# RWKV block inverses in a hybrid decoder layer: dense matmuls placed between the two groups of first products

## The chip, the cores and the metric

The kernel runs on one core of one Trainium2 chip. The metric is the device time of one execution in microseconds (us), the median of three runs; lower is better. One further execution was recorded by the hardware profiler, and the views of the profile and the trace are of that one. In the views, PE is TensorE (matmuls), PEld its weight loads, DVE is VectorE, ACT is ScalarE, POOL is GpSimd and SP is SyncE; PEclk is the share of full speed that TensorE's clock was granted.

## What is computed

The reference is one decoder layer on 1024 tokens of width 1024: RWKV-7 time mixing and an indexer-selected sparse attention side by side, gated together, then a SwiGLU feed-forward part. The change lies in the time mixing, whose core is a recurrence over the tokens, for 8 heads of 64 channels each:

```python
def step(state, inp):
    r_t, d_t, k_t, v_t, kk_t, a_t = inp
    sa = jnp.einsum('bhij,bhj->bhi', state, -kk_t)
    state = (state * d_t[:, :, None, :]
             + sa[..., None] * (kk_t * a_t)[:, :, None, :]
             + v_t[..., None] * k_t[:, :, None, :])
    y_t = jnp.einsum('bhij,bhj->bhi', state, r_t)
    return state, y_t
```

## The kernel before

The tokens are worked on in two halves of 512. Weights and activations are split into a high and a low part, and a dense product is the sum of three matmuls per 128 rows of the contraction (`mm3`, lines 137 to 149: L142 and L143 with the high part of the weight, L147 with its low part). One such dense matmul covers 128 x 128 weights and 512 tokens. For every weight tile ScalarE makes the high part (L116) and VectorE the low part (L117), after a load of 512 KB (L123).

**The recurrence in chunks.** `rwkv(half, ...)` runs over the quarters q of 256 tokens, two in each half, and each quarter has four chunks of 64 tokens, taken as two pairs (pr), each of two chunks (pa). Inside a chunk the recurrence becomes a triangular system, whose matrix must be inverted for every one of the 8 heads. The 64 x 64 inverse is made of blocks of 32:

1. The matrices MT of all chunks are computed (L710 to L714), and their 32 x 32 diagonal blocks go through memory (`d_n`) into a layout in which one partition holds one block (N).
2. The substitution: a loop of 31 steps on VectorE (L748 to L753) inverts all diagonal blocks. The results go back through memory (`d_w`, L755 and L764) into the tile TT, and VectorE transposes the upper blocks into TZ (L767).
3. First products: for each pair pr, 16 matmuls of 32 x 32 (L781), which the trace records as 32, multiply the off-diagonal block by a diagonal inverse. ScalarE copies the result to TZ with two copies for each pair (L784).
4. `inner(0)` (L791, 32 records; copied by L794 into rhs) is independent of the inverses.
5. Second products (L802): for each pair the copy of step 3 times the other diagonal inverse; ScalarE copies the result with a changed sign into TT (L805). Now the inverse is complete, and the scan over the four chunks begins (L843, L862, L874).

**What fills the time.** TensorE's issue order is the order in which the program is written (`manual_schedule` for PE alone). All other work of TensorE stands in a queue of generators, `fill`. `pump(n)` adds n to a credit and takes steps from the queue until the credit is used up; a step of dense work counts as many credits as it has matmuls (mostly 4, in one order of the feed-forward part 7), so that the credit can fall below zero and the next call then brings less. `ticks(n, m)` pumps n in m parts and after each part takes one step of a second generator, `beside`, the search for the attention's thresholds (L1008, and between its two passes L1030 and L1032). The calls before the first products cover the substitution:

```python
ticks((209, 231, 281, 232)[q], (13, 4, 10, 6)[q])
```

What the filler consists of differs by the quarter: in quarter 0 it is projections and gates (L142 to L147), in quarter 1 attention for the first half (`attend(0)`: logits L1109, their maximum on VectorE L1111, the exponent on ScalarE L1114, transposes L1144, values L1154, the end of a head pair with a store to `d_yb` at L1191) in turn with gates (L516, L517 and a store to `d_g`), in quarter 2 the merging of the branches (L1329, L1331, L248), in quarter 3 the feed-forward part (L1388 to L1392; L160 in its output order). At the start of quarter 2 the queue is emptied completely (`ready`).

**The other engines.** The order of VectorE, ScalarE, GpSimd and the DMA queues is made by a planner, which goes through the program with estimated durations and gives an engine that is free the earliest written instruction that it takes to be ready. On the chip each engine then keeps this order, so that an instruction that waits holds up all behind it. Small temporaries (`tmp`) rotate through four buffers: an instruction that writes a new one waits until the buffer's last user is done, which can be a store. Products that are not dense go to five PSUM banks (`mix`), dense ones to three (`acc`).

Of the kernel before, what the change touches and what calls it, by code (L numbers as in the profile page):

```python
# [51 lines left out]
def block_kernel(ctx: ExitStack, tc: tile.TileContext, ins: dict, outT: bass.AP, outR: bass.AP, stop=None, dbg=None):  # L52
# [56 lines left out]
    def mix():  # L109
        return psM.tile([128, HT], F32, tag="mix", name="mix")  # L110
# [66 lines left out]
    def pump(n):  # L177

        credit[0] += n
        while credit[0] > 0 and fill:  # L180
            try:
                credit[0] -= abs(next(fill[0]))
            except StopIteration:
                fill.popleft()
        if not fill:
            credit[0] = 0
# [3 lines left out]
    def ticks(n, m):  # L190

        for i in range(m):
            pump(n * (i + 1) // m - n * i // m)
            next(beside[0], None)
# [353 lines left out]
    def rwkv(half, p, consts, ready=None, settled=None):  # L548
# [5 lines left out]
        for q in range(2 * half, 2 * half + 2):  # L554
# [217 lines left out]
                             d_bs[q][e].rearrange("c s -> (c s)").partition_broadcast(64))  # L772
            bon = v
            G.tensor_tensor(bon, v, bsp, op=ALU.mult)
            ticks((209, 231, 281, 232)[q], (13, 4, 10, 6)[q])
            both = [(h, pa, 64 - 64 * pa, 64 * pa) for h in range(8) for pa in range(2)]
            hd = [(h, h // 2, slice((h % 2) * 64, (h % 2) * 64 + 64), slice(h * 64, h * 64 + 64)) for h in range(8)]
            for pr in range(2):
                ps = mix()
                for h, pa, ba, kb in both:  # L780
                    T.matmul(ps[ba + 32:ba + 64, h * 32:(h + 1) * 32], MT[2 * pr + pa][ba:ba + 32, h, ba + 32:ba + 64],  # L781
                             TZ[ba:ba + 32, 0, pr, h, :], start=True, stop=True)
                for ba in (64, 0):
                    A.activation(TZ[ba + 32:ba + 64, 1, pr, :, :],  # L784
                                 ps[ba + 32:ba + 64, 0:256].rearrange("p (h t) -> p h t", h=8), AF.Copy)

            def inner(pr):
                ps = mix()
                for h, pa, ba, kb in both:
                    hc = hd[h][3]  # L790
                    T.matmul(ps[ba:ba + 64, hc], MT[2 * pr + pa][kb:kb + 64, h, ba:ba + 64],  # L791
                             UV[pr][kb:kb + 64, pa, hc], start=True, stop=True)
                rhs = p.tile([128, 512], F32, tag="rhs", name="rhs")
                A.activation(rhs, ps, AF.Copy)  # L794
                return rhs
# [956 lines left out]

    fill.append(att0())
    rwkv(0, rp, consts)
    zps, z0, f0, merging = [], [], [], []

# [10 lines left out]
    def settled():  # L1767

        next(merging[0])
        fill.append(chain(merging[0], ffn(0, zps[0][1], z0, f0)))  # L1770

    rwkv(1, rp, consts, ready, settled)
    wq[0] = SY
    sz0, zp0 = zps[0]
# [114 lines left out]
```

## Time and profile before

| what | value |
|---|---|
| median of three runs | 1706.21 us (1706.05 to 1706.52) |
| profiled execution | 1709.14 us, of it 1707.2 us span from the first to the last instruction |
| TensorE busy | 1686.1 us, 99% of the span |
| VectorE, ScalarE, GpSimd busy | 1180.9, 896.4, 97.3 us |
| mean granted clock of TensorE | 0.996 |
| first products of quarters 0 to 3 begin at | 426.5, 575.5, 739.4 and 895.0 us |

The times in all rows of the timeline are us from the start of the span: start, busy time, engine, line, operation, output and inputs, shapes and count, and in brackets the engine's idle time just before with what ended it. Rows merge equal instructions that follow each other, and a matmul's busy time includes the part in which the next one already runs, so that rates are read from starts. In a view by stretches, each engine has its busy time and, in brackets, its instructions, and then come the granted clock, the share of the DMA engines and the GB/s. In the view of waits a row has the total, the number and the longest.

### The profile page before, as it was taken

Reading aid. Unit: us, or ns where it says so; the run is one execution under the profiler, and the core shown is the slowest. Engines: PE = TensorE matmul, PEld = TensorE weight load, DVE = VectorE, ACT = ScalarE, POOL = GpSimd, SP = SyncE. Lnnn points to the kernel's source line nnn. Section 1 sums busy time; section 2 is a strip of 40 time slices with the busy share of each in tenths; the row PEclk is TensorE's granted clock in tenths of the full one; section 3 lists DMA queues with packets and bytes.
Section 4 is the critical chain, followed back from the end, with each engine's and each line's share of the span. In section 5 each row is a group of like instructions: output and inputs, shape, how many; then the busy total and the mean of one; then the engine's idle time right before and its main releaser. Section 6 shows DMA issues by size and latency. Waiting matters only on the chain.

```text
span 1707.2 us, 28295 instructions
## 1 busy us (share of the span) xinstructions
PE 1686.1 (99%) x10802; PEld 1419.4 (83%) x10802; DVE 1180.9 (69%) x2305; ACT 896.4 (53%) x1727; POOL 97.3 (6%) x107
## 2 busy tenths in 40 slices
PE   9999999999999999999999999999999999999998
PEld 8888888878878777878787888878888899899998
DVE  6789889967567458957886655535564885675764
ACT  6365998453554588755334365533323544353452
POOL 0000000000021110000200110000000000000002
PEclk9999999999999899999999999999999999999999
DMA  6542334436257525653343633244455344524532
GB/s 220 178 136 91 98 104 149 147 108 181 98 177 213 153 95 170 207 171 109 106 123 97 213 128 120 76 154 166 145 185 187 113 156 131 183 95 144 169 113 99
DMA packets 142231, 243.58 MB, mean 143 GB/s; under 512 B 48864, under 2 KB 71072, under 8 KB 141968
## 3 DMA queue, kind: packets, MB, share of 16 engines
q1 hardware_dynamic: 119360, 170.76, 31.3%
q10 hardware_dynamic: 16128, 48.60, 8.5%
q0 software_dynamic: 6608, 22.42, 4.2%
q8 instruction: 85, 1.39, 0.3%
q14 instruction: 50, 0.41, 0.1%
HBM read 188.73 MB, written 53.00 MB: 142 GB/s over the span
## 4 chain that ended last, share of the span: by engine, by line
PE 87%; DVE 5%; DMA 3%; ACT 2%; issue 1%; POOL 1%; SPq 0%; ACTq 0%; POOLq 0%; DVEq 0%
PE acc L142 18%; PE acc L147 18%; PE acc L143 18%; PE acc L160 3%; PE mix L1597 3%; PE mix L1595 3%; PE mix L1594 3%; PE mix L1154 2%; PE mix L958 2%; PE mix L1144 2%; PE mix L1128 1%; PE acc L417 1%; DVE wlo L117 1%; PE mix L142 1%; PE acc L1597 1%
## 5 line engine op out<-in xcount | busy, mean ns | idle before, releaser
L117 DVE TENSOR_TENSOR wlo<-wst,whi 128x1024 fp32r<-128x1024 f32 (+1 forms) x203 | 246.4, 1216 | 181.2 <-PE acc L147 73.9
L116 ACT ACTIVATE whi<-wst 128x1024 fp32r<-128x1024 f32 (+1 forms) x203 | 212.3, 1048 | 185.7 <-PE acc L143 137.1
L142 PE MATMUL acc<-zhi,whi 128*128 128x512 f32 x400 | 158.8, 397 | 0.0
L143 PE MATMUL acc<-zlo,whi 128*128 128x512 f32 x400 | 156.1, 390 | 0.0
L142 PE MATMUL acc<-u1hi,whi 128*128 128x512 f32 x320 | 128.5, 401 | 0.0
L143 PE MATMUL acc<-u1lo,whi 128*128 128x512 f32 x320 | 125.5, 392 | 0.0
L142 PE MATMUL acc<-u0hi,whi 128*128 128x512 f32 (+1 forms) x320 | 122.8, 386 | 0.0
L143 PE MATMUL acc<-u0lo,whi 128*128 128x512 f32 (+1 forms) x320 | 121.3, 382 | 0.0
L147 PE MATMUL acc<-zhi,wlo 128*128 128x512 f32 x400 | 103.1, 395 | 0.0
L142 PE MATMUL acc<-fhi,whi 128*128 128x512 f32 x234 | 91.9, 393 | 0.6 <-ACT whi L116 0.5
L143 PE MATMUL acc<-flo,whi 128*128 128x512 f32 x234 | 91.1, 390 | 0.0
L142 PEld LDWEIGHTS acc<-zhi,whi 128*128 128x128 f32 x400 | 75.1, 188 | 16.9 <-issue 1.8
L143 PEld LDWEIGHTS acc<-zlo,whi 128*128 128x128 f32 x400 | 75.2, 188 | 14.7
L147 PEld LDWEIGHTS acc<-zhi,wlo 128*128 128x128 f32 x400 | 73.6, 188 | 15.6 <-issue 1.2
L147 PE MATMUL acc<-u1hi,wlo 128*128 128x512 f32 x320 | 82.5, 398 | 0.0
L147 PE MATMUL acc<-u0hi,wlo 128*128 128x512 f32 (+1 forms) x320 | 78.7, 384 | 0.0
L1008 ACT ACTIVATE junkl<-kept,z 128x1024 int8<-128x1024 int16 (+1 forms) x64 | 69.4, 1084 | 4.6 <-DVE kept L977 4.4
L142 PEld LDWEIGHTS acc<-u1hi,whi 128*128 128x128 f32 x320 | 60.3, 189 | 12.7 <-issue 0.9
L147 PEld LDWEIGHTS acc<-u1hi,wlo 128*128 128x128 f32 x320 | 59.6, 190 | 12.8 <-issue 0.9
L142 PEld LDWEIGHTS acc<-u0hi,whi 128*128 128x128 f32 x320 | 60.2, 188 | 11.9 <-issue 0.4
L143 PEld LDWEIGHTS acc<-u1lo,whi 128*128 128x128 f32 x320 | 60.5, 189 | 11.3
L143 PEld LDWEIGHTS acc<-u0lo,whi 128*128 128x128 f32 x320 | 60.2, 188 | 11.0
(455 smaller groups left out, 4041.0 us busy)
## 6 DMA issues: line engine op xcount, KB each, us to landing
wst<-in_w_ffn_in SPq DMA_DIRECT2D x72, 512.0 KB, 3.8
wst<-in_w_in ACTq DMA_DIRECT2D x36, 512.0 KB, 3.9
wst<-in_w_in SPq DMA_DIRECT2D x25, 512.0 KB, 4.3
wst<-in_w_fo SPq DMA_DIRECT2D x25, 512.0 KB, 3.5
h<-in_xT SPq DMA_DIRECT2D x32, 256.0 KB, 5.2
d_g<-tmp ACTq DMA_DIRECT2D x32, 256.0 KB, 2.8
k<-d_k POOLq DMA_DIRECT2D x16, 512.0 KB, 5.8
tmp<-d_g SPq DMA_DIRECT2D x32, 256.0 KB, 3.0
```

The source lines that it names most:

```text
L116: A.activation(hi, x, AF.Copy)
L117: V.tensor_tensor(lo, x, hi.bitcast(F32), op=ALU.subtract)
L142: T.matmul(ps, whi[:, wk + k, :], ahi[:, ak + k, tok], start=k == 0, stop=False)
L143: T.matmul(ps, whi[:, wk + k, :], alo[:, ak + k, tok], start=False, stop=False)
L147: T.matmul(ps, wlo[:, wk + k, :], ahi[:, ak + k, tok], start=False, stop=k == nk - 1)
L160: T.matmul(ps, w[:, k, :], a[:, k, tok], start=k == 0 and j == 0, stop=k == nk - 1 and j == 2)
L958: T.matmul(ps[:, :w], iq[:, h, :], ik[:, i, c:c + w], start=i == 0, stop=i == 1)
L1008: A.activation(junka[:, :n], y, AF.Sign, bias=z[:, i:i + 1], accum_out=cnt[:, i:i + 1])
L1144: T.transpose(ps[:, j * 128:(j + 1) * 128], L[:, (c + j) * 128:(c + j + 1) * 128], ident)
L1594: T.matmul(ps, whi[:, k, :], ahi[:, k, :], start=opens and k == 0, stop=False, skip_group_check=True)
L1595: T.matmul(ps, whi[:, k, :], alo[:, k, :], start=False, stop=False, skip_group_check=True)
L1597: T.matmul(ps, wlo[:, k, :], ahi[:, k, :], start=False, stop=k == 3, skip_group_check=True)
```

## The change

Two lines. Behind each of the two groups of first products, after its two copies on ScalarE are written, `pump(4)` is called, in every quarter. The pumping before the first products falls from 209, 231, 281 and 232 to 202, 223, 281 and 226, that is by 7, 8, 0 and 6. The number of parts in which it is done stays.

```diff
-            ticks((209, 231, 281, 232)[q], (13, 4, 10, 6)[q])
+            ticks((202, 223, 281, 226)[q], (13, 4, 10, 6)[q])
             both = [(h, pa, 64 - 64 * pa, 64 * pa) for h in range(8) for pa in range(2)]
             hd = [(h, h // 2, slice((h % 2) * 64, (h % 2) * 64 + 64), slice(h * 64, h * 64 + 64)) for h in range(8)]
             for pr in range(2):
                 ps = mix()
                 for h, pa, ba, kb in both:
                     T.matmul(ps[ba + 32:ba + 64, h * 32:(h + 1) * 32], MT[2 * pr + pa][ba:ba + 32, h, ba + 32:ba + 64],
                              TZ[ba:ba + 32, 0, pr, h, :], start=True, stop=True)
                 for ba in (64, 0):
                     A.activation(TZ[ba + 32:ba + 64, 1, pr, :, :],
                                  ps[ba + 32:ba + 64, 0:256].rearrange("p (h t) -> p h t", h=8), AF.Copy)
+                pump(4)
```

No matmul is added or removed: what is pumped at one place is missing from the queue at a later one.

## The prediction

> **What bounds the kernel now.** I read the page first: its busy table, then its chain.
>
> ```profile
> span 1707.2 us, 28295 instructions
> PE 1686.1 (99%) x10802; PEld 1419.4 (83%) x10802; DVE 1180.9 (69%) x2305; ACT 896.4 (53%) x1727; POOL 97.3 (6%) x107
> ...
> PE 87%; DVE 5%; DMA 3%; ACT 2%; issue 1%; POOL 1%; SPq 0%; ACTq 0%; POOLq 0%; DVEq 0%
> ```
>
> TensorE is busy 99% of the span and its issue order is fixed by the program. Every dense matmul is run once in either kernel, so the change can only gain where TensorE stands still or is slowed, and only lose where it adds such time. Hence the view of waits next, for TensorE alone.
>
> ```profile
> PE mix L802 <- ACT TZ L784: 2.7, 3, 2.3
> PE mix L710 <- DVE MT L714: 1.9, 2, 1.1
> ...
> PE mix L781 <- DVE TZ L767: 0.7, 1, 0.7
> ```
>
> The longest of all its waits lies at the place of the change: the second products (L802) wait for the copies (L784) of the first products (L781), once for 2.3 us. The other row that the change can reach is L781 waiting for a transpose. So I read TensorE's timeline at each of the four places. Quarter 0 is the undisturbed pattern:
>
> ```profile
> 425.96 0.39 PE L142 MATMUL acc<-u0hi,whi 128*128 128x512 f32 x1
> 426.19 0.39 PE L143 MATMUL acc<-u0lo,whi 128*128 128x512 f32 x1
> 426.50 1.20 PE L781 MATMUL mix<-TZ,MT 32*32 32x32 f32 x64
> 427.63 1.15 PE L791 MATMUL mix<-UV,MT 64*64 64x64 f32 x32
> 428.71 0.50 PE L142 MATMUL acc<-u0hi,whi 128*128 128x512 f32 x1
> ...
> 429.83 1.20 PE L802 MATMUL mix<-TT,TZ 32*32 32x32 f32 x64
> ...
> 432.00 0.50 PE L142 MATMUL acc<-u0hi,whi 128*128 128x512 f32 x1
> ```
>
> The step from one start to the next is what counts, since the durations overlap: a dense matmul takes 0.23 us (425.96 to 426.19), 64 first products 1.13, the inner products (L791) 1.08, L802 and L843 together 2.17. The four dense ones behind L791 take 1.12 (428.71 to 429.83), not 0.92: going from small products to dense and back costs about 0.2 us.
>
> Quarter 1 holds the long wait, so here TensorE, ScalarE and the granted clock:
>
> ```profile
> 574.23 0.88 PE L1154 MATMUL mix<-pt,v 128*64 128x128 f32 x12
> 575.04 0.50 PE L1109 MATMUL mix<-k,q 128*128 128x256 f32 x2
> 575.47 1.20 PE L781 MATMUL mix<-TZ,MT 32*32 32x32 f32 x64
> ...
> 581.21 2.31 PE L802 MATMUL mix<-TT,TZ 32*32 32x32 f32 x64 [2.33 <-ACT TZ L784]
> ...
> 585.35 0.79 PE L142 MATMUL acc<-u1hi,whi 128*128 128x512 f32 x1
> ```
> ```profile
> 574.54 0.71 ACT L1030 ACTIVATE tmp<-kept,top 128x512 f32<-128x512 int16 x1
> ...
> 576.05 0.51 ACT L1114 ACTIVATE L<-L,mx 128x256 f32<-128x256 f32 x1 [0.80 <-DVE mx L1111]
> ...
> 578.91 1.84 ACT L1030 ACTIVATE tmp<-kept,top 128x512 f32<-128x512 int16 x3 [2.26 <-DMA d_yb<-tmp]
> 580.78 1.57 ACT L784 ACTIVATE TZ<-mix 32x256 f32<-32x256 f32 x4
> ```
> ```profile
> 576.00:580.00 4.00, 2.88 (x79) 2.24 (x72) 0.95 (x4) 1.69 (x4) 0.00 (x0) 1.00 0.99 377
> 580.00:584.00 4.00, 2.71 (x70) 2.51 (x70) 1.44 (x3) 3.84 (x10) 0.00 (x0) 0.58 0.08 26
> 584.00:588.00 4.00, 4.00 (x22) 3.17 (x21) 1.15 (x4) 2.71 (x7) 0.00 (x0) 0.50 0.00 2
> 588.00:592.00 4.00, 4.00 (x27) 3.06 (x28) 0.43 (x2) 3.60 (x10) 1.20 (x2) 0.64 0.23 66
> ```
>
> The first products take their 1.13 us, to 576.6, but their copies begin at 580.78. ScalarE keeps the order that it was given: three L1030 stand ahead of L784, and the first of them waits until 578.91 for a store (d_yb) that has to land before its buffer is free, while the DMA share of that stretch is 0.99. TensorE idles 2.33 us, and then the granted clock falls to half: L802 and L843 take 4.14 us here (581.21 to 585.35) against 2.17 in quarter 0. Lost clock over the three stretches: 4 x (0.42 + 0.50 + 0.36) = 5.1 us, an estimate from above, since TensorE partly stands in it. Bounds for the drop: at least the 2.0 us of those two groups, at most 5.1; I take 4.8, as nearly all that follows until 591 is work at TensorE's own pace.
>
> [...]
>
> Quarter 2 has two smaller stalls:
>
> ```profile
> 739.44 0.75 PE L781 MATMUL mix<-TZ,MT 32*32 32x32 f32 x34
> 740.92 0.69 PE L781 MATMUL mix<-TZ,MT 32*32 32x32 f32 x30 [0.73 <-DVE TZ L767]
> ...
> 745.88 1.11 PE L843 MATMUL mix<-S,AR 64*128 64x64 f32 x16
> ```
> ```profile
> 740.43 0.43 DVE L767 STREAM_TRANSPOSE TZ<-TT 32x256 f32<-32x256 f32 x1 [1.52 <-DMA TT<-d_w]
> ```
> ```profile
> 743.63 1.57 ACT L784 ACTIVATE TZ<-mix 32x256 f32<-32x256 f32 x4
> ```
>
> The second group waits for the last transpose, which waits for its DMA until 740.43; later L802 waits for copies that begin at 743.63. Quarter 3 has no wait at all:
>
> ```profile
> 895.04 1.20 PE L781 MATMUL mix<-TZ,MT 32*32 32x32 f32 x64
> ...
> 897.25 1.88 PE L160 MATMUL acc<-flo,whi 128*128 128x512 f32 x7
> 899.06 1.20 PE L802 MATMUL mix<-TT,TZ 32*32 32x32 f32 x64
> ```
>
> **The change part by part.** No matmul is added or removed. Credits before the first products fall by 7, 8, 0 and 6, and 8 come back behind the two groups, so behind them the filler stands 1, 0, 8 and 2 credits ahead, within its quarter. Three terms.
>
> *New borders.* Each quarter gets two more islands of filler between small products. Price of one: 1.12 - 4 x 0.23 = 0.2 us, the nearest row there is. It is not below zero, since the filler itself costs its usual time. Quarter 0: 0.4. Quarter 2: 0.4. Quarter 3: its filler comes in pieces of seven (L160 x7 above), so 4 + 4 + 4 credits buy two islands where one stood: 0.2. Quarter 1: paid inside the wait for ScalarE, so 0 while that wait is there, 0.4 if it goes. Sum 1.0; its range is 0.5 to 1.4, by half the price and by two islands everywhere.
>
> [...]
>
> *Quarter 2.* The first group starts at 739.44 as before (281 is unchanged) and takes 0.6. Four dense then run to 739.44 + 0.6 + 1.1 = 741.1; the second group's transpose ends at 740.86, so its wait is covered with 0.3 us to spare. Second group 0.6, four dense 1.1, inner products 1.1, four dense 1.1: L802 is reached at about 745.1. By the quoted ScalarE row all four copies end at 745.20 and the first pair at 744.4, so both groups find theirs. L843 then starts at 746.2 instead of 745.88, 0.3 later, but with eight dense matmuls more behind it, worth 8 x 0.23 = 1.8: a gain of 1.5 us, islands already paid. Without the cover (transpose or copies later by over a microsecond) it falls towards the bare islands, -0.4.
>
> *Quarter 1.* Filler here is attention as well as dense work. L1154 and L1109 carry 3 and 2 credits and the two pieces ahead of them 4 each, so seven credits fewer take out just those two items: L781 starts about 1.2 us earlier, with L1154 behind the first group and L1109 behind the second. TensorE still has the same work ahead of L802 and reaches it near 579.2. ScalarE's row decides: L1030 is written ahead of L784 in both kernels and the planner takes ready work in that order, so the copies remain behind the store that lands at 578.91. L802 starts near 581.2 as before: 0.
>
> *What could be uncovered.* Starting L781 up to 8 x 0.23 = 1.8 us sooner needs its transposes:
>
> ```profile
> 423.09 0.42 DVE L767 STREAM_TRANSPOSE TZ<-TT 32x256 f32<-32x256 f32 x1
> ...
> 566.64 1.35 DVE L767 STREAM_TRANSPOSE TZ<-TT 32x256 f32<-32x256 f32 x3
> ...
> 890.46 0.42 DVE L767 STREAM_TRANSPOSE TZ<-TT 32x256 f32<-32x256 f32 x1
> ```
>
> They end at 423.5, 568.0 and 890.9; L781 would start at 424.7, 574.3 and near 893.4. All hold, quarter 0 by 1.2 us. No semaphore wait is added, but copies of the second group are now written behind four credits of filler, so ScalarE may place that filler's work ahead of them; they have over 3 us until L802 in quarters 0 and 3. Filler's own weight loads, splits and stores on the ScalarE and SyncE queues keep their order and move by up to 1.8 us against the inverse. Behind the second quarter the filler runs 8 credits ahead, which shifts its VectorE bursts against the next norms; the waits there (L710, 1.9 us in two) can grow or shrink by about a microsecond, and I take 0.
>
> Sum: +0.4 (quarter 0) + 0 - 1.5 (quarter 2) + 0.2 (quarter 3) = -0.9 us. The islands of quarter 2 are inside its -1.5. The profiled execution took 1709.14 us, 1.9 beyond its span; with the sum it would take 1708.2. The median of the three runs is 2.9 us lower, 1706.21, and so the forecast is 1705.3. Whether those runs have the clock drop is not shown; they agree within 0.5 us, so probably all or none.
>
> **The rivals.**
>
> *A, the copies get past L1030.* L1030's first one was started while L1114 was not ready, and then L1114 was placed ahead of the rest, so the rest may not have been ready in the planner's eyes. With L781 1.2 us earlier, L784 can take that slot; if both pairs do, wait and drop go: -0.9 + 0.4 - 2.3 - 4.8 = -7.6, 1698.6 us. For it: ScalarE's gap at 576.05. Against: the second pair is written behind the filler. 0.17.
>
> *B, wait stays, clock doesn't fall.* TensorE reaches L802 near 579.2, so it idles 1.9 instead of 2.33 us: -0.9 - 4.8 = -5.7, 1700.5 us. The trace halves the clock after 2.33 us and does not after 0.73 (quarter 2), so 1.9 lies between, nearer to the first. [...] 0.13.
>
> *C, slower: copies of the second group late in another quarter.* If ScalarE sets the shifted filler, or a wait like L1030's, ahead of them, L802 waits there and the clock falls. The copies of a pair take 0.8 us and L802 comes 3.3 us after its group, so it decides from 2.5 us of delay on; quarter 1 shows that 4 us occur. Price as in quarter 1, 2.3 + 4.8: 1705.3 + 7.1 = 1712.4 us. 0.12.
>
> *D, no cover in quarter 2* (its stalls are not in every run, or move along): bare islands, +1.0, 1707.2 us. 0.10.
>
> **How the numbers follow.** The forecast gets 0.48. 0.2% of this time is 3.4 us, about what a measurement of this kernel can tell from no change. Faster by more: A and B, 0.30. Within: forecast and D, 0.58. Slower: C, 0.12. The forecast's own range is 1703.8 to 1707.6, by the bounds of the islands and a microsecond at the norms; the range for 8 in 10 takes in B and reaches to A, about half of which it leaves out with C: 1699.0 to 1708.5.
>
> **What would show it.** Right: L781 in two groups of 32 with filler between; quarter 2 without the 0.73 us wait, its L843 with eight more dense behind it at 746; in quarter 1 L1030 still ahead of L784 on ScalarE, L802 near 581 and a clock below 1.00 after it; islands at 1.1 us for four dense. Wrong: the copies directly behind their products in quarter 1, a clock of 1.00 throughout, or L802 waiting in quarter 0 or 3.

## The result and the profile after

The kernel after takes 1723.58 us (median of six runs, 1717.57 to 1725.12), the kernel before on the same chip 1707.3 us (1706.05 to 1710.24): a ratio of 1.0085, 95% interval 1.0066 to 1.0104. It is slower by 16 us, outside the predicted range. The profiled execution took 1723.18 us. Two runs of an experiment and two of the kernel before beside the experiments, of 1848.04 to 9491.47 us, were disturbed (two of them at a granted clock of 0.849) and are left out of all figures. Lines from 787 on are one higher in the kernel after.

The first lines of its page, and its view of waits for TensorE (total, number, longest, in us):

```profile
span 1721.1 us, 28296 instructions
...
PE 1693.6 (98%) x10802; PEld 1422.4 (83%) x10802; DVE 1183.6 (69%) x2305; ACT 899.8 (52%) x1727; POOL 94.8 (6%) x107
```
```profile
PE mix L710 <- DVE MT L714: 2.6, 3, 1.4
PE acc L1350 <- ACT yhi L116: 1.8, 1, 1.8
PE mix L875 <- ACT UV L866: 1.7, 2, 0.9
PE mix L655 <- ACT nrT L649: 1.4, 1, 1.4
...
PE acc L143 <- DVE zlo L117: 1.2, 1, 1.2
PE mix L863 <- DVE rhs L854: 1.2, 1, 1.2
PE mix L255 <- DVE sacc L249: 1.1, 1, 1.1
```

L802 (now L803) and L781, the two rows that the change was about, no longer stand among the long waits. In their place are single waits of 0.9 to 1.8 us at lines that the diff does not touch: the norms (L655, L710), the start of the merge (L1350), the scan (L863, L875) and the feed-forward part (L255, L143).

At the place of the change things went as forecast. TensorE in quarter 2, and the two steps that had stalled it (VectorE's last transposes, ScalarE's copies):

```profile
740.76 0.69 PE L781 MATMUL mix<-TZ,MT 32*32 32x32 f32 x32
741.38 0.50 PE L142 MATMUL acc<-mhi,whi 128*128 128x512 f32 x1
...
742.51 0.69 PE L781 MATMUL mix<-TZ,MT 32*32 32x32 f32 x32
...
746.48 1.20 PE L803 MATMUL mix<-TT,TZ 32*32 32x32 f32 x64
747.61 0.66 PE L844 MATMUL mix<-S,AR 64*128 64x64 f32 x8
```
```profile
739.93 0.90 DVE L767 STREAM_TRANSPOSE TZ<-TT 32x256 f32<-32x256 f32 x2 [2.29 <-DMA TT<-d_w]
```
```profile
743.60 1.57 ACT L784 ACTIVATE TZ<-mix 32x256 f32<-32x256 f32 x4
```

No wait is left. From L781 to L844 it is 6.85 us (747.61 - 740.76), before 6.44 (745.88 - 739.44), with eight dense matmuls more inside: 8 x 0.23 - 0.41 = 1.4 us gained where 1.5 was forecast. But quarter 2 began its inverse 1.3 us later than before, and the profiled execution as a whole lost 13.9 us of span.

Quarter 1, on ScalarE, TensorE and in the stretches behind it (busy times, then granted clock, DMA share, GB/s):

```profile
577.58 1.34 ACT L1031 ACTIVATE tmp<-kept,top 128x512 f32<-128x512 int16 x2 [1.07 <-DMA d_yb<-tmp]
579.17 0.62 ACT L1031 ACTIVATE tmp<-kept,top 128x384 f32<-128x384 int16 x1 [0.25 <-DVE kept L1033]
579.81 1.57 ACT L784 ACTIVATE TZ<-mix 32x256 f32<-32x256 f32 x4
```
```profile
580.64 1.49 PE L803 MATMUL mix<-TT,TZ 32*32 32x32 f32 x62 [0.15 <-ACT TZ L784]
```
```profile
580.00:584.00 4.00, 3.54 (x83) 2.83 (x82) 1.10 (x4) 3.80 (x11) 0.00 (x0) 1.00 0.06 19
584.00:588.00 4.00, 4.00 (x23) 2.76 (x24) 1.29 (x5) 3.93 (x11) 1.19 (x2) 0.57 0.10 34
```

The order is the forecast one, the copies behind what was L1030. The store landed at 577.58 in place of 578.91, so the 2.33 us of wait are gone; the clock fell all the same, for 3.41 us in place of 10.24.

Where the loss begins can be read at L655 in quarter 1's norm, 66 us ahead of that inverse. ScalarE and TensorE, first after, then before:

```profile
508.15 0.63 ACT L517 ACTIVATE tmp<-tmp 128x512 f32<-128x512 f32 x1 [2.61 <-DVE tmp L516]
508.68 0.36 ACT L649 ACTIVATE nrT<-mix 16x256 fp32r<-16x256 f32 x1
```
```profile
509.09 0.73 PE L655 MATMUL mix<-nrT,ind 16*128 16x256 f32 x4 [1.42 <-ACT nrT L649]
```
```profile
505.16 0.36 ACT L649 ACTIVATE nrT<-mix 16x256 fp32r<-16x256 f32 x1
507.27 0.34 ACTq L123 DMA_DIRECT2D wst<-in_w_in  x1
507.87 0.63 ACT L517 ACTIVATE tmp<-tmp 128x512 f32<-128x512 f32 x1 [2.35 <-DVE tmp L516]
```
```profile
507.74 0.73 PE L655 MATMUL mix<-nrT,ind 16*128 16x256 f32 x4
```

The planner turned two steps of ScalarE round: L517, which waits 2.61 us for VectorE, now stands ahead of the small copy of nrT (L649), and L655 needs that copy. What shifts the filler at this place is the one surplus credit of quarter 0 (its two islands lie ahead too): between L647 and L655 TensorE has eight dense matmuls, before it had twelve, since one more piece of four was drawn ahead.

The next step is the start of the first merge, TensorE and then ScalarE:

```profile
678.62 1.03 PE L1350 MATMUL acc<-yhi,whi 128*128 128x512 f32 x2 [1.77 <-ACT yhi L116]
```
```profile
673.79 1.95 ACT L116 ACTIVATE yhi<-ylo 128x512 fp32r<-128x512 f32 x3 [3.23 <-DMA ylo<-d_ya]
```

TensorE begins the merge 2.6 us sooner than before (674.30 against 676.94) and reaches the first weight product behind it, L142, 1.3 us later (683.82 against 682.56): 3.9 us go here, in the wait and in 3.41 us of half clock from 679.95 on. ScalarE's splits (L116) wait for a load of d_ya, and L732 stands ahead of two of them.

Two more of this size follow. One is at the second merge's operands, where L142 waits 0.73 us and L143 1.18 until 1365.66, with 3.41 us of half clock from 1366.03 on: 3.5 us. The other is in quarter 3's norm and ahead of it. TensorE and the stretches around two of its waits:

```profile
794.59 1.02 PE L255 MATMUL mix<-kc,sacc 128*128 128x2 f32 x8 [1.11 <-DVE sacc L249]
...
842.76 1.17 PE L710 MATMUL mix<-AR,BK 64*128 64x128 f32 x16 [1.38 <-DVE MT L714]
```
```profile
794.00:798.00 4.00, 3.41 (x19) 3.15 (x20) 2.54 (x6) 0.00 (x0) 1.01 (x1) 0.75 0.00 0
798.00:802.00 4.00, 4.00 (x19) 3.44 (x19) 1.57 (x4) 2.52 (x7) 0.00 (x0) 0.82 0.13 33
842.00:846.00 4.00, 2.60 (x28) 2.41 (x29) 4.00 (x8) 0.63 (x1) 0.00 (x0) 0.72 0.42 130
846.00:850.00 4.00, 4.00 (x22) 3.78 (x19) 1.57 (x4) 1.77 (x3) 0.00 (x0) 0.50 0.60 126
```

These two waits cost a second time, as the clock falls behind them: 4 x (0.25 + 0.18) = 1.7 us at the first, 4 x (0.28 + 0.50) = 3.1 us at the second. In the mean over runs, time x (1 - mean granted clock) is 9.5 us after, and 5.3 to 5.8 in the runs of the kernel before beside the experiments: by this estimate about 4 of the 16 us are lost clock and 12 are waits and islands.

### The profile page after: what moved, and what is told of

Its sections match the earlier page's. It is cut to its first block, busy times and chain, and to the rows that moved or that the text cites. A ratio compares the mean times of both kernels' runs of the same rounds, so it can differ in the third digit from the quotient of the medians.

```text
span 1721.1 us, 28296 instructions
## 1 busy us (share of the span) xinstructions
PE 1693.6 (98%) x10802; PEld 1422.4 (83%) x10802; DVE 1183.6 (69%) x2305; ACT 899.8 (52%) x1727; POOL 94.8 (6%) x107
## 4 chain that ended last, share of the span: by engine, by line
PE 63%; DVE 5%; ACT 2%; POOL 1%; issue 1%; DMA 0%; POOLq 0%; SPq 0%; DVEq 0%; ACTq 0%
PE acc L142 13%; PE acc L143 12%; PE acc L147 12%; PE acc L160 4%; PE mix L1598 3%; PE mix L1596 3%; PE mix L1595 3%; PE mix L1155 2%; PE mix L1145 2%; PE mix L1129 1%; PE acc L1598 1%; PE acc L1595 1%; PE acc L1596 1%; DVE wlo L117 1%; PE mix L844 1%
## 5 line engine op out<-in xcount | busy, mean ns | idle before, releaser
L116 ACT ACTIVATE whi<-wst 128x1024 fp32r<-128x1024 f32 (+1 forms) x203 | 212.3, 1048 | 196.2 <-PE acc L143 140.5
L142 PE MATMUL acc<-zhi,whi 128*128 128x512 f32 x400 | 159.4, 398 | 0.7 <-ACT zhi L116 0.7
L143 PE MATMUL acc<-zlo,whi 128*128 128x512 f32 x400 | 156.3, 391 | 1.2 <-DVE zlo L117 1.2
L142 PE MATMUL acc<-u1hi,whi 128*128 128x512 f32 x320 | 128.0, 400 | 0.0
L143 PE MATMUL acc<-u1lo,whi 128*128 128x512 f32 x320 | 125.3, 391 | 0.0
L142 PE MATMUL acc<-u0hi,whi 128*128 128x512 f32 (+1 forms) x320 | 123.0, 387 | 0.0
L143 PE MATMUL acc<-u0lo,whi 128*128 128x512 f32 (+1 forms) x320 | 121.3, 382 | 0.0
L142 PE MATMUL acc<-fhi,whi 128*128 128x512 f32 x234 | 92.3, 394 | 0.9 <-ACT whi L116 0.9
L143 PE MATMUL acc<-flo,whi 128*128 128x512 f32 x234 | 91.2, 390 | 0.0
L142 PEld LDWEIGHTS acc<-zhi,whi 128*128 128x128 f32 x400 | 75.5, 189 | 18.1 <-issue 2.1
L143 PEld LDWEIGHTS acc<-zlo,whi 128*128 128x128 f32 x400 | 75.4, 188 | 16.3 <-DVE zlo L117 1.5
L142 PEld LDWEIGHTS acc<-u1hi,whi 128*128 128x128 f32 x320 | 60.1, 188 | 12.9 <-issue 1.3
L142 PEld LDWEIGHTS acc<-u0hi,whi 128*128 128x128 f32 x320 | 60.2, 188 | 11.9 <-issue 0.4
L143 PEld LDWEIGHTS acc<-u1lo,whi 128*128 128x128 f32 x320 | 60.2, 188 | 11.3
L143 PEld LDWEIGHTS acc<-u0lo,whi 128*128 128x128 f32 x320 | 60.2, 188 | 10.9
```

The lines of the kernel that those rows point to most:

```text
L116: A.activation(hi, x, AF.Copy)
L142: T.matmul(ps, whi[:, wk + k, :], ahi[:, ak + k, tok], start=k == 0, stop=False)
L143: T.matmul(ps, whi[:, wk + k, :], alo[:, ak + k, tok], start=False, stop=False)
```

## The experiments

The change has three separable parts: islands (the pieces of filler between the small products), their place, and surplus credits (1, 0, 8, 2) that move all later filler ahead. Experiments 1 to 6 separate them, 7 and 8 apply a surplus without any island. Ratios are to the kernel before, run beside them on the same chip, with 95% intervals; it took 1707.46 us beside experiments 1 to 4, 1707.42 beside 5 to 8, 1707.10 beside 9 to 12 and 1706.41 beside 13 to 16.

**1, 2 and 3: islands without surplus, the surplus without islands (drawn ahead of the inverses), the change with its surplus repaid.**

```diff
 # e1_net_zero: pump(4) as in the change
+ticks((201, 223, 273, 224)[q], (13, 4, 10, 6)[q])
 # e2_shift_only: no islands
+ticks((210, 231, 289, 234)[q], (13, 4, 10, 6)[q])
 # e3_end_repaid: the change, and at the quarter's end
+pump((61, 62, 54)[q])      # q3: ticks(60, 2)
```

> The same two pieces of filler behind the first products, but eight credits fewer ahead of them in every quarter, so that the filler stands behind the inverse where it stood in the kernel before. Theory 1 (the surplus: the changed kernel is slow because 1, 0, 8 and 2 credits more have been pumped behind the inverses, which moves the later norms, scans and boundaries of the filler against their producers): 1702 to 1709 us, since only the borders (about 1 us) and the gain in quarter 1 (3.5 us between the two traces) are left. Theory 2 (any edit reorders ScalarE and VectorE all over the program, and the loss comes from that): 1712 to 1722 us, with waits at far places such as L1350 (1.8 us) and the operands behind the second merge (1.9 us). Theory 3 (the borders themselves are dear): 1718 us or more.

> No filler between the groups; only the surplus of 1, 0, 8 and 2 credits, pumped ahead of the first products. Theory 1 (surplus): 1716 to 1726 us, as the changed kernel, or some 3 us more since quarter 1 keeps its wait and its halved clock. Theory 2 (any edit): 1712 to 1722 us, at other places. Theory 3 (borders): within 2 us of the kernel before.

> The changed kernel, with the surplus taken back at the end of the same quarter (61, 62, 54 and 60 in place of 62), so that the next quarter starts where it did before. Theory 1 in the form that the surplus acts beyond its own quarter (norms of quarter 3, the operands behind the second merge, together 6 to 7 us between the two traces): 1714 to 1718 us. If the surplus acts within its own quarter: 1720 us or more. Theory 2: no saying, 1712 to 1724 us.

Measured: e1 1713.2 us, 1.003 (1.0017 to 1.0043); e2 1730.16, 1.0124 (1.0099 to 1.0148); e3 1714.18, 1.0034 (1.0021 to 1.0047). The surplus without islands is the worst of all, and the change with the surplus taken back loses 7 instead of 16 us. So the surplus costs most, and the islands are not the larger part.

**4, 5 and 6: one quarter at a time.**

```diff
 # e4_q1_only: ticks (209, 223, 281, 232)
+if q == 1: pump(4)
 # e5_q2_only: ticks as before, so a surplus of eight stays
+if q == 2: pump(4)
 # e6_q2_repaid: e5, and at the quarter's end
+pump((62, 62, 54)[q])
```

> The change in quarter 1 alone, where it is balanced (8 fewer, 8 back). Theory 1 (surplus): the 3.5 us that quarter 1 gains between the two traces, and no loss: 1702 to 1706 us. Theory 2 (any edit): the 3.9 us lost at the start of the first merge (L1350 waits 1.8 us for ScalarE, and the clock falls) come with it: 1706 to 1712 us. Theory 3: 1707 us.

> The change in quarter 2 alone: 281 ahead as before, four and four credits behind the groups, so a surplus of 8 from there on. Theory 1 (surplus of quarter 2, carried into quarter 3): 1715 to 1720 us, most of the 16 us. Theory 1b (the surpluses of quarters 0 and 3 matter as much): 1709 to 1713 us. Theory 3 (borders): 1708 us.

> As the run with quarter 2 alone, with the 8 credits taken back at the end of the quarter (54 in place of 62). Theory 1: the wait for the transpose (0.7 us) and that for the copies are covered and nothing follows: 1705.5 to 1707.5 us, 1 us below the kernel before. Theory 2 (any edit reorders what follows, as quarter 1 alone did with 1714 us): 1709 to 1714 us.

Measured: e4 1714.04 us, 1.0031 (1.0015 to 1.0046); e5 1712.92, 1.0032 (1.002 to 1.0043); e6 1706.63, 0.999 (0.9979 to 1.0001). Quarter 2's islands alone measured -0.8 us, within the interval of no change; their surplus costs 6.3 (1712.92 - 1706.63). Quarter 1's islands cost 6.6 although their credits are balanced. Its new wait lies in the next norm, at 656.85; the second fence is that place in e10 below, which has no islands in quarter 1:

```profile
656.85 0.33 PE L631 MATMUL mix<-kc,nq 128*128 128x128 f32 x1 [1.27 <-DVE mx L1113]
```
```profile
653.89 0.38 PE L631 MATMUL mix<-kc,nq 128*128 128x128 f32 x2
```

Of the 5.8 us that e4's profiled execution is behind that of the kernel before, 1.5 arose ahead of its edit, 2.1 between 650 and 700 us (that norm and the merge's start) and 1.7 in quarter 2's inverse.

How the surplus of quarter 2 costs can be read at L255, a sum over the merge's result. TensorE, then VectorE, in e5 and in e6:

```profile
790.85 1.12 PE L255 MATMUL mix<-kc,sacc 128*128 128x2 f32 x8 [1.25 <-DVE sacc L249]
```
```profile
790.02 0.68 DVE L249 TENSOR_TENSOR sacc<-sacc,tmp 128x512 f32<-128x512 f32 x1
```
```profile
790.55 1.04 PE L255 MATMUL mix<-kc,sacc 128*128 128x2 f32 x8
```
```profile
789.80 0.68 DVE L249 TENSOR_TENSOR sacc<-sacc,tmp 128x512 f32<-128x512 f32 x1
```

VectorE ends its sum at nearly the same time, at 790.70 and 790.48. With the surplus TensorE is there at 789.60 (790.85 - 1.25) and waits; in e6 the products of L815 and L816 (789.22 to 790.55) still stand ahead of L255, in e5 they come behind it.

**7 and 8: a surplus and nothing else.**

```diff
 # e7_surplus8
+pump((62, 62, 70)[q])
 # e8_surplus1: one credit, at quarter 0's end
+pump((63, 62, 62)[q])
```

> No filler between groups and none more ahead of them; the kernel before with 70 in place of 62 at the end of quarter 2. Theory 1 in its sharpest form (8 credits too many at the start of quarter 3 do it, whatever the inverse looks like): 1714 to 1720 us. If it needs the inverse of quarter 2 as well: 1706 to 1710 us.

> The kernel before with 63 in place of 62 at the end of quarter 0: one credit, the smallest surplus there is. Theory 1 (each shift is paid by its size against the norm that it meets): 1707 to 1709 us, with the wait of 1.4 us for L649 in quarter 1's norm at most. Theory 2 (any edit): 1710 us or more, with waits in quarters 2 and 3.

Measured: e7 1711.4 us, 1.0025 (1.0007 to 1.0043), with runs from 1705.15 to 1718.03; e8 1718.21, 1.006 (1.0046 to 1.0074). One credit of some 10,800 matmuls costs 10.8 us. Its rows in the view of waits:

```profile
PE mix L655 <- ACT nrT L649: 2.8, 2, 1.4
PE acc L1349 <- ACT yhi L116: 2.5, 1, 2.5
```

The same turn at L649 as in the change, once more in the next norm, and a wait at the merge's start. With 10.8 and e5's 5.5 the change's 16.3 seemed explained. Experiment 9 took that sum apart.

**9 and 10: the change without the one credit, and without quarter 1.**

```diff
 # e9_q0_balanced: the change with
+ticks((201, 223, 281, 226)[q], (13, 4, 10, 6)[q])
 # e10_no_q1: ticks (201, 231, 281, 224), pump((62, 62, 54)[q]) at the end
+if q != 1: pump(4)
```

> The whole change, but its first quarter hands out one credit less at the ticks (201 for 202), so that what the islands pump is what the ticks lack there; the surpluses of q2 (eight) and q3 (two) stay. If the one surplus credit of q0 is what costs most (10.8 us alone in e8), some 9 us of the change's 16 go and the time is 1711 to 1716 us; PE's wait of 1.42 us at L655 in q1's norm is gone. Rival: the flips come from the islands themselves or from q2's and q3's surplus, and the one credit is chance: then the time stays at 1719 us or more.

> Islands in q0, q2 and q3, each quarter balanced: ticks 201, 231, 281 and 224, the eight surplus credits of q2 taken back at its end (54 for 62), no island in q1. If what costs is the phase of the filler in the stages behind an inverse and q1's own islands, nothing is left but the islands' 0.2 us each and q2's gain near 1 us: 1706 to 1708 us. Rival: an island that only lies elsewhere already turns the planner's order somewhere: 1710 us or more, with a wait at a line of a norm or of the merge that the kernel before does not show.

Measured: e9 1724.79 us, 1.0101 (1.0085 to 1.0117); e10 1707.77, 1.0001 (0.9988 to 1.0014). My theory of the one credit falls: the rival's 1719 or more came. L655 waits 0.4 us in e9, in place of 1.4, and the time is no better, since L631 now waits 1.3 us as in e4 and quarter 3's norm waits as in e5. Inside the change the credit costs nothing; alone it costs 10.8: the prices do not add. e10 settles the islands: three quarters of them, balanced, cost nothing that can be measured.

**11 and 12: the turned order taken back.**

```diff
 # e11_credit_pinned: e8 with this; e12_pin_control: before with this
+with tc.high_priority():
+    A.activation(nrT, ps[0:16, 0:256], AF.Copy)
```

> The kernel before with one surplus credit at the end of q0, as in e8, and the copy of nrT (L649) put ahead by priority, so that it stands before L517 on ScalarE. If that one turn of order is what the credit costs, PE's wait of 1.42 us at L655 goes and with it what follows from it: 1708 to 1712 us, to be read against e12. Rival: the credit costs by many turns of order, of which this is only the first: 1715 us or more, with the waits at the merge's start and behind q2 still there.

> Control for e11: the kernel before with the copy of nrT (L649) put ahead by priority and no surplus credit. If the priority alone does nothing to the time where nothing waited: 1705 to 1710 us. Rival: the priority itself turns the order elsewhere, in q2's norm: 1712 us or more, and e11 is then read against this.

Measured: e11 1717.52 us, 1.0065 (1.0049 to 1.008); e12 1706.59, 0.9997 (0.9986 to 1.0008). In e11 nrT stands ahead of L517 again, and L655 waits half as long:

```profile
508.87 0.37 ACT L650 ACTIVATE nrT<-mix 16x256 fp32r<-16x256 f32 x1 [2.39 <-PE acc L143]
509.15 0.61 ACT L517 ACTIVATE tmp<-tmp 128x512 f32<-128x512 f32 x1
```
```profile
509.30 0.73 PE L656 MATMUL mix<-nrT,ind 16*128 16x256 f32 x4 [0.68 <-ACT nrT L650]
```

The time stays. L631 (1.2 us), L844 (1.5) and the merge's operands wait as in e8, so that turn was one of many.

**13 and 14: quarter 2's surplus with the late sum put ahead.**

```diff
 # e13_q2_pinned: e5 with this; e14_q2_repaid_pinned: e6 with this
+with tc.high_priority() if (half, d) == (0, 7) else nullcontext():
     V.tensor_tensor(h[:, d, :], h[:, d, :], ps, op=ALU.add)
+    sq.add(d)
```

> q2's islands alone with their surplus of eight, as in e5 (1712.9), and VectorE's last sum of squares of the merge's first half (L249, with the addition to h before it, L1331) put ahead by priority: it then stands right behind L905, in place of behind three of the six steps that make zlo, some 2.6 us earlier. If what the surplus costs begins with PE reaching L255 eight dense matmuls (1.8 us) sooner while that sum stays where it was (1.25 us of wait there and a window of half clock of 3.41 us behind it), the wait at L255 and the window are gone and 2 to 3 us of e5's 5.5 with them: 1709.5 to 1711, to be read against e14. If L710's wait in q3's norm (1.38 us, a window of 6.83 us) comes of the same delay, it goes too: 1706 to 1708. Rival: the L255 wait is only the place at which a loss made elsewhere shows, and PE waits later instead: 1712 or more.

> Control for e13: q2's islands with the surplus taken back at the quarter's end, as in e6 (1706.6), with the same priority on the merge's last addition and sum of squares. Without a wait at L255 to take away, the priority is worth nothing: 1705 to 1708.5 us. Rival: the priority moves other steps of VectorE (the scan's state behind it): 1710 us or more.

Measured: e13 1709.5 us, 1.001 (0.9998 to 1.0023); e14 1705.9, 0.9993 (0.9982 to 1.0004). VectorE and TensorE in e13:

```profile
790.33 0.68 DVE L249 TENSOR_TENSOR sacc<-sacc,tmp 128x512 f32<-128x512 f32 x1
790.93 2.73 DVE L1341 SCALAR_TENSOR_TENSOR zlo<-h,par,zhi 128x512 fp32r<-128x512 f32 x4
```
```profile
791.74 0.95 PE L255 MATMUL mix<-kc,sacc 128*128 128x2 f32 x8
```

The sum now ends 0.7 us ahead of L255, the wait is gone, and e13's median is 3.4 us below e5's (1712.92), about the wait and the clock behind it: 1.25 + 3.41/2 = 3.0 us (e5's record has half clock for 3.41 us from 791.64 on, e13's none there). The two intervals just touch, so the size is rough; 3.6 us against e14 remain. L710 still waits 1.38 us, and there the clock still falls (0.81 in 836 to 840, 0.76 in 840 to 844). At L255 the mechanism is shown: the surplus costs because TensorE reaches a place that another engine does not reach sooner.

**15 and 16: the sign turned.**

```diff
 # e15_deficit1
+pump((61, 62, 62)[q])
 # e16_deficit8
+pump((62, 62, 54)[q])
```

> The kernel before with one credit less at q0's end (61 for 62): e8 with the sign turned. If a lead of PE's filler over the other engines is what costs, a lag costs nothing there: 1704 to 1709 us. Rival: any shift by a piece turns the planner's order in q1's norm somewhere and the order of before is the better one by choice: 1711 us or more.

> The kernel before with eight credits less at q2's end (54 for 62): e7 with the sign turned (e7 was 1711.4). If the lead costs (PE at L255 before VectorE's L249), the lag costs nothing: 1704 to 1709 us, no wait at L255 above the 0.5 us of before. Rival: either sign costs, since the steps behind were placed for this phase: 1711 us or more.

Measured: e15 1725.14 us, 1.0102 (1.0082 to 1.0122); e16 1714.26, 1.0041 (1.0026 to 1.0056). Both rivals came: a lag costs at least as much as a lead (18.7 us against 10.8 for one credit, 7.9 against 4.0 for eight). (Of the 8.2 us that e16's profiled execution is behind, 1.9 arose ahead of its edit.) In e15, TensorE in quarter 1's norm:

```profile
518.13 1.09 PE L1109 MATMUL mix<-k,q 128*128 128x128 f32 x4 [2.67 <-issue]
```

That wait is in no other kernel; L874 (2.3 us) and L1349 (3.5 us in three) wait behind it. So being ahead of VectorE is only one way to lose: any shift by a piece gives the planner another list to order, and each of the four shifts tried alone (e7, e8, e15, e16) ran slower than the order before. Why the order of before is the better one in all four is not shown.

## Why the prediction was wrong

**The step that failed** is the last one of "What could be uncovered": filler "1, 0, 8 and 2 credits ahead, within its quarter", moved waits that "can grow or shrink by about a microsecond, and I take 0". Both halves were wrong. Nothing pays the credits back at a quarter's end: the queue is emptied at the start of quarter 2 and then not before the filler runs out. And the term is not a microsecond: surplus alone, or lag alone, measured +4 (e7), +7.9 (e16), +10.8 (e8) and +18.7 us (e15), never a gain. The change holds two sources of loss: quarter 1's islands, +5.7 to +6.7 where the surplus is taken back or absent (e1, e3, e4), and the surplus of quarters 2 and 3, some 11 more (e9's 17.7 against e3's 6.7). Of that, quarter 2's eight credits alone cost 6.3 (e5 against e6); quarter 3's two were not run alone. I had limited the planner's part to the copies (rival C) and the engines' part to L710.

**Quarter 1 at 0** was wrong too, in the term and in its basis. The 2.33 us with the clock drop were one draw of many. Seven other kernels run the same instructions in the same order up to there:

| profiled execution | before | e5 | e6 | e7 | e12 | e13 | e14 | e16 |
|---|---|---|---|---|---|---|---|---|
| longest wait at the second products (us) | 2.33 | 0.80 | 1.01 | 0.19 | 2.43 | 1.49 | 0.55 | 1.06 |
| half clock around them (us) | 10.24 | 3.41 | 0 | 0 | 6.83 | 6.83 | 3.41 | 3.41 |

In e6 and e7 ScalarE's L1030 did not wait for the store at all. My guess that the runs have that drop all or none is refuted, and rivals A and B priced 4.8 us of lost clock where these eight lose 2.1 us on average (half of each stretch). And the balanced islands, which I took as free inside that wait, cost 6.6 us alone; the added wait at L631 (1.27 us) and a wait at the merge's start (0.64 us) are part of it, while what turned there, for want of a run with L631 mended, stays open. (231 to 223 is eight credits, not the seven of that paragraph; the two items moved as it says.)

**What held.** The islands: in quarter 0 from L781 to the first dense matmul behind L844 it took 7.88 us (432.20 - 424.32) against 5.50, of it 1.84 for eight dense: 0.54 for two islands, 0.4 forecast. Quarter 3 filled in pieces of seven:

```profile
901.66 0.69 PE L781 MATMUL mix<-TZ,MT 32*32 32x32 f32 x32
902.28 1.88 PE L160 MATMUL acc<-flo,whi 128*128 128x512 f32 x7
904.09 0.69 PE L781 MATMUL mix<-TZ,MT 32*32 32x32 f32 x32
```

L803 then started at 907.60, which makes 5.94 us against 4.02, of it 7 x 0.23 more dense work: 0.3 for the island, 0.2 forecast. Quarter 2's cover held with 1.4 of 1.5 us. The sum of the islands, -0.9 us with quarter 2's gain in it, agrees with e6 (-0.8) and e10 (+0.7), which can't be told from no change. Rival C named the side, but not the mechanism: no copy of L784 was late in another quarter.

## What to carry to other kernels

Where a filler queue feeds a planner, price a change in three parts: its work, its place, and the shift that it leaves behind; here the work was worth about a microsecond, the place nothing in three quarters and 6 to 7 us in one, and the shift up to 19. Build the variant that pays the credits back before anything is concluded about the place. And before a gain is read from a long wait in one profile, look for that wait in a second execution of the same instructions, as it may be one draw of many.

## What the runs showed of the hardware

In the records of these profiles half clock lasts 3.41, 6.83 or 10.24 us at a stretch, one to three times 3.413 (but for the last of an execution, 5.75 us before and 5.82 after, which reaches past the span's end), and the starts in one execution lie whole multiples of 3.413 us apart (after: 584.38, 679.95 and 796.01 us, 28 and 62 steps on). Little idled ahead of some of them: behind 1.11 us at L255 the record has half clock from 796.01 on, and in quarter 1 from 584.38 on, behind waits of 0.15 and 0.20 us among 32- and 64-wide products (0.57 in 584 to 588). The length of a wait alone did not decide: behind 1.42 us at L655 and 1.18 us at L863 in the same execution the clock stayed (1.00 in 508 to 516 and in 932 to 940), as it did in e6 behind 1.01 us among the same small products (0 us of half clock in the table above).

The clock also goes with most of the spread. In 23 runs of the kernel before (experiments 9 to 12) the time goes from 1703.05 us, at a mean granted clock of 0.998, to 1716.57, at 0.993. Of the 13.5 us between these two, 8.6 are time x (1 - clock), 3.4 against 12.0 us. Over all 23 it goes from 1.7 to 12.0 us and follows the time with a correlation of 0.96, in the three other groups of such runs with 0.88 to 0.93. How long TensorE must idle for the clock to fall was not tried.
